# Dot products of the modulation vectors: their products into the next weight tile's low half, at a set rate per tile and stage

## The chip, the cores and the metric

The kernel runs on one core of a Trainium2 chip. The metric is the device time of one execution in microseconds. The profile shows five engines: PE (TensorE, matmuls; PEld its weight loads), DVE (VectorE), ACT (ScalarE), POOL (GpSimd) and SP (SyncE, which issues most DMAs).

## What is computed

Two transformer blocks over 256 tokens of width 1024, all in fp32. What matters here are the adaptive modulation vectors of the second block: for each of its two layers, six vectors of 1024 come from one row vector `c` and a matrix of 1024 x 6144, and for the context a shorter set from `c_ctx`.

```python
silu_c = jax.nn.silu(c)
silu_cc = jax.nn.silu(c_ctx)
for i in range(DEPTH_2):
    sh1, sc1, g1, sh2, sc2, g2 = jnp.split((silu_c @ ada_w[i] + ada_b[i])[:, None, :], 6, axis=-1)
    hx = modulate(xs, sh1, sc1)            # h * (1 + scale) + shift
    ...
    csh1, csc1, ... = jnp.split(silu_cc @ ada_w[i] + ada_b[i], 6, axis=-1)
    hc = modulate(cs, csh1, csc1)
```

The rest are matrix products with large weights: attention projections, a feed-forward pair `up` and `down`, and per layer of the second block an expert table `u`, `v` of 128 tiles each.

## The kernel before

The weights stream from HBM as tiles of 128 x 1024 fp32 (512 KB), in one fixed order, the list `items` (lines 123 to 130). The class `Stream` (line 78) does three things for a tile: `dma` issues its load on SP into one of three `raw` buffers (line 89); `split` writes a high half on ACT (line 103) and the rest, raw minus high, on DVE (line 104) into one of three `hi` and three `lo` buffers; `next` hands the pair to a matrix product, after it has issued loads up to four tiles ahead and splits up to one tile ahead. Each product is then three matmul passes: high by high, high by low, low by high.

The stages around the change, in order of time: cqkv, qk, uq, ukv, vg (4, 8, 2, 1, 8 tiles) with attention between them; five tiles of kc; wout (8) with the residual add and norm of lines 642 to 648 behind it; three more tiles of kc; up (44 tiles, `gemm_T` at line 229, each followed by `conv`, line 657, whose two DVE steps at 662 and 663 read PSUM); down (22, `gemm_N` at line 247) with the same kind of add and norm (lines 680 to 688); vc; the projections abq, abgu, abk, abgv; a second vc; then the two layers, each with u and v tiles (matmuls at line 1095 and 1158). In v, each tile also has its activation tile split into `w` (lines 1146 and 1147).

The modulation products are done on DVE, not on PE: the matrix lies transposed in HBM as tiles of 128 output columns by 1024, and one `scalar_tensor_tensor` (line 338) multiplies such a tile by the silu row and sums along the row, a dot product for each of 128 partitions. There are 16 for the context (`actx`), 48 for layer 0 (`ada0`) and 48 for layer 1 (`ada1`). The products themselves are not needed, only the sums; before, they overwrite the loaded tile. `ada_gen` (line 332) is a generator: one step issues the next load into one of three slots, the next step does the dot of the tile before. `fill(n)` (line 206) takes `n` such steps, with a fraction carried along in `debt`; the matrix products call it after each tile with `nfill` (1.3 in the first stage, 1 in wout, 0.75 in up, 1.5 in down, 1 later), so two steps make one dot. `fill_until` finishes what is left where the sums are needed.

The order in which instructions stand in each engine's queue is not the order of the program text alone. The kernel is built with `schedule_with_timeline_sim=True` (line 1333): a planner orders each queue by program order among what it reckons to be ready, and puts waits where a buffer or a value is needed. A step whose inputs are ready early can be moved ahead of program text before it. Each engine then works its queue in order.

Of the kernel before, what the change touches and what calls it, by code (L numbers as in the profile page):

```python
# [17 lines left out]
ALU = mybir.AluOpType  # L18
# [16 lines left out]
DA0, DA1 = 2, 13  # L35
NF1 = 1.3
TWO_PI = 2.0 * math.pi
# [8 lines left out]
def tile_two_blocks(ctx: ExitStack, tc: tile.TileContext, T, out):  # L46
    nc = tc.nc
# [9 lines left out]
    def nm(s):  # L57
        uid[0] += 1
        return f"{s}{uid[0]}"
# [18 lines left out]
    class Stream:  # L78
# [14 lines left out]
        def split(self, upto):  # L93
            while self.nsp < min(upto, len(self.items)):
                i = self.nsp
                w = self.items[i][1].shape[1]
                r = self.raw.pop(i)
                if i in self.own:
                    h, l = self.own.pop(i)[:2]
                else:  # L100
                    h = hi_pool.tile([128, 1024], F32R, tag="hi", name=nm("hi"))
                    l = lo_pool.tile([128, 1024], F32R, tag="lo", name=nm("lo"))
                ACT.activation(h[:, :w], r[:, :w], AF.Copy)  # L103
                DVE.tensor_sub(l[:, :w], r[:, :w], h[:, :w].bitcast(F32))  # L104
                self.hl[i] = (h, l)
                self.nsp += 1
# [95 lines left out]
    fillers = deque()  # L202

    debt = [0.0]

    def fill(n=1, tag="b"):
        debt[0] += n
        n, debt[0] = int(debt[0]), debt[0] % 1.0
        while n > 0 and fillers:
            try:  # L210
                next(fillers[0][1])
                n -= 1
            except StopIteration:
                fillers.popleft()

    def fill_until(key):
        while any(k == key for k, _ in fillers):
            try:
                next(fillers[0][1])
            except StopIteration:  # L220
                fillers.popleft()
# [6 lines left out]

    def gemm_T(name, n, xt, evac, tag="b", per=8, nfill=0, first=0):
# [17 lines left out]
    def gemm_N(name, nk, width, segs, xt, tag, per=1, nfill=0, tail=1, sqrt=False, evac=None, own=(), turn=0):  # L247

# [5 lines left out]
        for t0 in range(0, nt - tail + 1):  # L254
# [4 lines left out]
            for n in range(2):  # L259
# [71 lines left out]

    def ada_gen(layer, tiles, row, dst, slot):

        ahead = deque()

        def dot():
            c, r = ahead.popleft()
            DVE.scalar_tensor_tensor(r, r, 1.0, row(), op0=ALU.mult, op1=ALU.mult, accum_out=dst[:, c : c + 1])  # L338
            if c % 8 == 7:
                d = dst[:, c - 7 : c + 1]  # L340
                DVE.tensor_add(d, d, col(f"ada_b{layer}", c - 7, c + 1))
# [12 lines left out]

# [19 lines left out]
    with ExitStack() as b1:  # L374
# [9 lines left out]
        with ExitStack() as at:  # L384
# [42 lines left out]

            acc = gemm_N("cqkv", 8, 416, [(0, 416)], views(hT), "b", per=2, nfill=NF1)
            ssq = sm(4)
# [42 lines left out]

            acc_qk = gemm_N("qk", 8, 1024, seg2, views(hT), "a", nfill=NF1)


            def uq_evac(n, acc):
                for i in range(2):
# [4 lines left out]

            gemm_N("uq", 2, 768, [(0, 384), (384, 768)], views((cT[:, 0], cT[:, 1])), "b", tail=2, nfill=NF1,
                   evac=uq_evac)
# [7 lines left out]

            gemm_N("ukv", 1, 1024, seg2, ((lambda k: cT[:, 0, 2]), (lambda k: cT[:, 1, 2])), "b", nfill=NF1,
                   evac=ukv_evac)
# [80 lines left out]

            acc = gemm_N("vg", 8, 1024, seg2, views(hT), "a", nfill=NF1)
            vr = pa.tile([128, 1024], F32, name="vr", tag="cv").rearrange("p (n f) -> p n f", n=2)
# [58 lines left out]
        silu[0] = silu_row(p1.tile([128, D], F32, name="silu"), 0)  # L636
        fillers.append(("ada0", ada_gen(0, range(48), lambda: silu[0], adac[:, 0], slot)))
        acc = gemm_N("wout", 8, 1024, seg2, views(hT), "a", nfill=1, tail=3, sqrt=True)
        junk = p1.tile([128, D], F32, name="junk1")
# [34 lines left out]

        gemm_T("up", 44, viewsT(hT), conv, nfill=0.75)
        acc = gemm_N("down", 22, 1024, [(0, 512), (512, 1024)], views(gT), "a", nfill=1.5, tail=3, sqrt=True)
        fnw = p1.tile([128, D], F32, name="fnw")
        bcast_row(fnw, T["final_norm_w"])
        xn = p1.tile([128, 2, D], F32, name="xn2", tag="xn")
        for n in range(2):  # L680
            for i in range(2):
# [14 lines left out]
             scr=lambda: pf.tile([128, 2, 256], F32, tag="t", name=nm("t")))  # L696
        acc = gemm_N("vc", 8, 1024, [(0, 512), (512, 1024)], views(chT), "a", nfill=1)
        for n in range(2):
# [74 lines left out]
    with ExitStack() as b2:  # L773
# [53 lines left out]
        gv = pb.tile([128, 2, 512], F32, name="gv")  # L827
        acc_q = gemm_N("abq", 8, 1024, seg2, xv8, "a", nfill=1)
        acc_u = gemm_N("abgu", 8, 512, [(0, 512)], xv8, "b", per=2, nfill=1)
        qk_rope(acc_q, 0)  # L830
        acc_k = gemm_N("abk", 8, 1024, seg2, xv8, "a", nfill=1)
        for n in range(2):
            ACT.activation(gu[:, n], acc_u[n][0], AF.Gelu_apprx_tanh)
        acc_v = gemm_N("abgv", 8, 512, [(0, 512)], xv8, "b", per=2, nfill=1)
        qk_rope(acc_k, 1)
# [81 lines left out]
        for i in range(LEAD):  # L917
            scores(i)
        acc = gemm_N("vc", 8, 1024, seg2, xv8, "a", nfill=1)
        for n in range(2):  # L920
# [28 lines left out]
    def peer(layer, hT, nxt):  # L949
        with ExitStack() as pe_ctx:  # L950
# [159 lines left out]
            if layer == 0:  # L1110
# [9 lines left out]
                silu1 = silu_row(places[3], 0)  # L1120
                fillers.append(("ada1", ada_gen(1, range(48), lambda: silu1, adac[:, 1], place)))
            acc = [[bank("a") for _ in range(2)] for _ in range(2)]
            flat1 = lambda a, b: A1[:, a:b].rearrange("p j t -> p (j t)")
            for j0 in range(0, 129 - TAIL):
# [26 lines left out]
                for n in range(2):  # L1151
# [194 lines left out]
```

## Time and profile before

| | us |
|---|---|
| median of three timed runs | 2383.87 (2383.73 to 2384.34) |
| the profiled execution | 2381.28 |
| its span, first to last instruction | 2379.5 |
| PE busy in the span | 2257.6 (95%) |
| DVE busy | 1839.2 (77%) |
| ACT busy | 1323.3 (56%) |

A profile's busy time of PE comes from pipelined matmuls with modelled ends, so it is read together with the number of matmuls in a stretch. PEclk is the granted clock of TensorE as a share of its full speed. The idle time of an engine counts only where another engine waits for what it does next, so a stage is read by what ends the last wait in it.

### The profile page before, as it was taken

How to read it: one execution, taken by the hardware profiler on the slowest of the kernel's cores; microseconds unless marked ns; L12 is line 12 of the kernel's file. 1: busy time of each engine (PE TensorE's matmuls, PEld its weight loads, DVE VectorE, ACT ScalarE, POOL GpSimd, SP SyncE). 2: the span in 40 equal slices, each digit the busy share in tenths (PEclk: the TensorE clock that was granted, in tenths of full speed). 3: DMA queues.
4: the chain of work that ended last, by engine and by line, in shares of the span. 5: the costliest groups of instructions: out<-in, count | busy, mean ns of one | idle time of the engine just before them, and what ended most of it. 6: DMA issues, size and time to landing. Idle time of an engine off the chain costs nothing.

```text
span 2379.5 us, 40021 instructions
## 1 busy us (share of the span) xinstructions
PE 2257.6 (95%) x14710; PEld 2017.7 (85%) x14710; DVE 1839.2 (77%) x3679; ACT 1323.3 (56%) x2509; POOL 309.3 (13%) x359
## 2 busy tenths in 40 slices
PE   6886999999899999999999998799999999999998
PEld 6785898776699999998778887699999999888886
DVE  7879875768699957898996666789967898555565
ACT  4634554456444548876555553435547877555553
POOL 1000110211112401121000002411321112000000
PEclk9998999999899999999999999899999999999999
DMA  9559655750445554446995663444554444555663
GB/s 320 177 182 325 224 185 173 238 173 28 138 165 176 180 184 160 153 159 253 367 343 195 221 205 132 142 151 165 182 187 162 157 156 156 187 191 187 209 219 104
DMA packets 124309, 452.80 MB, mean 190 GB/s; under 512 B 13904, under 2 KB 13920, under 8 KB 123728
## 3 DMA queue, kind: packets, MB, share of 16 engines
q1 hardware_dynamic: 121104, 438.23, 53.2%
q0 software_dynamic: 3008, 12.02, 1.5%
q8 instruction: 115, 1.88, 0.3%
q14 instruction: 82, 0.67, 0.1%
HBM read 449.14 MB, written 1.05 MB: 189 GB/s over the span
## 4 chain that ended last, share of the span: by engine, by line
PE 82%; DVE 9%; DMA 3%; issue 2%; ACT 2%; POOL 1%; SPq 0%; DVEq 0%; ACTq 0%; POOLq 0%
PE pb L1158 29%; PE pb L273 10%; PE pb L1095 10%; PE pb L1096 9%; PE pb L1097 9%; PE pb L240 3%; PE pb L241 3%; PE pb L242 3%; DVE lo L104 2%; DVE araw L338 1%; PE pb L1073 1%; PE pb L1074 1%; DMA araw<-in_ada_wT 1%; POOL oh L1025 1%; ACT hi L103 1%
## 5 line engine op out<-in xcount | busy, mean ns | idle before, releaser
L104 DVE TENSOR_TENSOR lo<-raw,hi 128x1024 fp32r<-128x1024 f32 (+1 forms) x700 | 868.6, 1242 | 280.4 <-ACT hi L103 279.3
L103 ACT ACTIVATE hi<-raw 128x1024 fp32r<-128x1024 f32 (+1 forms) x700 | 739.5, 1058 | 557.4 <-PE pb L1096 245.5
L1095 PE MATMUL pb<-hTh,hi 128*128 128x256 f32 x2048 | 589.2, 288 | 1.4 <-ACT A L1099 1.4
L1097 PE MATMUL pb<-hTh,lo 128*128 128x256 f32 x2048 | 578.5, 283 | 0.6 <-DVE lo L104 0.6
L1096 PE MATMUL pb<-hTl,hi 128*128 128x256 f32 x2048 | 578.7, 283 | 0.0
L1158 PE MATMUL pb<-hi,w 128*128 128x512 f32 x1952 | 535.0, 395 | 1.1 <-ACT w L1146 1.1
L1158 PEld LDWEIGHTS pb<-hi,w 128*128 128x128 f32 x1952 | 366.4, 188 | 90.3 <-ACT w L1146 1.6
L1095 PEld LDWEIGHTS pb<-hTh,hi 128*128 128x128 f32 x2048 | 391.8, 191 | 2.2 <-ACT A L1099 2.0
L1097 PEld LDWEIGHTS pb<-hTh,lo 128*128 128x128 f32 x2048 | 391.2, 191 | 1.4 <-DVE lo L104 1.3
L1096 PEld LDWEIGHTS pb<-hTl,hi 128*128 128x128 f32 x2048 | 392.0, 191 | 0.0
L1158 PE MATMUL pb<-lo,w 128*128 128x512 f32 x976 | 307.2, 395 | 1.4 <-DVE lo L104 1.3
L1146 ACT ACTIVATE w<-A 128x256 fp32r<-128x256 f32 x252 | 104.4, 417 | 263.2 <-PE pb L1158 260.1
L1158 PEld LDWEIGHTS pb<-lo,w 128*128 128x128 f32 x976 | 182.8, 188 | 47.3 <-DVE lo L104 3.5
L240 PE MATMUL pb<-hTh,hi 128*128 128x256 f32 x672 | 192.9, 290 | 17.7 <-DVE u L663 17.7
L241 PE MATMUL pb<-hTl,hi 128*128 128x256 f32 x672 | 194.7, 291 | 1.1 <-DVE hTl L314 1.1
L242 PE MATMUL pb<-hTh,lo 128*128 128x256 f32 x672 | 192.4, 288 | 0.9 <-DVE lo L104 0.9
L1147 DVE TENSOR_TENSOR w<-A,w 128x256 fp32r<-128x256 f32 x252 | 107.2, 427 | 99.0 <-PE pb L1158 96.7
L1070 ACT ACTIVATE oh<-oj,gf 128x128 f16<-128x128 f16 x512 | 162.7, 395 | 0.0
L240 PEld LDWEIGHTS pb<-hTh,hi 128*128 128x128 f32 x672 | 131.4, 197 | 19.6 <-issue 13.6
L1109 POOL TENSOR_TENSOR A<-A,tmp 128x4 f32<-128x4 f32 (+42 forms) x128 | 83.2, 650 | 447.7 <-ACT A L1081 447.7
L241 PEld LDWEIGHTS pb<-hTl,hi 128*128 128x128 f32 x672 | 131.8, 196 | 2.2 <-DVE hTl L314 2.2
L242 PEld LDWEIGHTS pb<-hTh,lo 128*128 128x128 f32 x672 | 131.7, 196 | 1.3 <-DVE lo L104 1.3
(435 smaller groups left out, 3090.0 us busy)
## 6 DMA issues: line engine op xcount, KB each, us to landing
raw<-in_u SPq DMA_DIRECT2D x256, 512.0 KB, 3.5
raw<-in_v SPq DMA_DIRECT2D x248, 512.0 KB, 4.2
araw<-in_ada_wT SPq DMA_DIRECT2D x64, 512.0 KB, 5.1
spare<-in_ada_wT SPq DMA_DIRECT2D x48, 512.0 KB, 5.4
raw<-in_up SPq DMA_DIRECT2D x44, 512.0 KB, 3.5
raw<-in_wq SPq DMA_DIRECT2D x32, 512.0 KB, 3.6
raw<-in_down SPq DMA_DIRECT2D x22, 512.0 KB, 3.5
raw<-in_vc SPq DMA_DIRECT2D x16, 512.0 KB, 3.5
```

The source lines that it names most:

```text
L103: ACT.activation(h[:, :w], r[:, :w], AF.Copy)
L104: DVE.tensor_sub(l[:, :w], r[:, :w], h[:, :w].bitcast(F32))
L240: PE.matmul(p, h[:, kk[1]], xh(done, k), start=(k == 0), stop=False)
L241: PE.matmul(p, h[:, kk[1]], xl(done, k), start=False, stop=False)
L242: PE.matmul(p, l[:, kk[1]], xh(done, k), start=False, stop=(k == per - 1))
L273: PE.matmul(acc[n][i][:, : b - a], w, r[:, s * width + a : s * width + b], start=(k == f0 and lhs is xh and r is h), stop=(k == f1 and lhs ...
L1070: ACT.activation(row(oh, c), row(oj, c), AF.Copy, scale=gf[:, t0 + c : t0 + c + 1])
L1095: PE.matmul(p, h[:, ks], xh(0, k), start=(k == 0), stop=False)
L1096: PE.matmul(p, h[:, ks], xl(0, k), start=False, stop=False)
L1097: PE.matmul(p, l[:, ks], xh(0, k), start=False, stop=(k == 7))
L1147: DVE.tensor_sub(wl, aj, wh.bitcast(F32))
L1158: PE.matmul(acc[n][i], lhs[:, ns], r[:, i * 512 : i * 512 + 512], start=(j == 0 and lhs is wh and r is h), stop=(j == 127 and lhs is wl))
```

## The change

The generator becomes an object whose `step` issues a load and, once three tiles are on the way, does the dot of the oldest, so one step is one dot and two loads run ahead. `fill` is called from `Stream.split`, before a tile is split, with the name of the tile's weight and the lo buffer that the tile is going to use; a table `PACE` gives the dots per tile by weight. The dot writes its products into that lo buffer instead of over its own input; the subtraction of line 104 then writes the buffer as before. The calls of `fill` behind the tiles go, and with them `nfill`. Weights that are not in the table (kc, wout, the second layer's, and u, pin and so on) get no dots.

```diff
-NF1 = 1.3
+PACE = {"cqkv": 1, "qk": 1, "uq": 1, "ukv": 1, "vg": 1, "up": 0.25, "down": 1.25,
+        "vc": 0.5, "abq": 1, "abgu": 1, "abk": 1, "abgv": 1, "v0": 0.5}
...
                     l = lo_pool.tile([128, 1024], F32R, tag="lo", name=nm("lo"))
+                fill(self.items[i][0], l)
                 ACT.activation(h[:, :w], r[:, :w], AF.Copy)
                 DVE.tensor_sub(l[:, :w], r[:, :w], h[:, :w].bitcast(F32))
...
-    def fill(n=1, tag="b"):
-        debt[0] += n
-        n, debt[0] = int(debt[0]), debt[0] % 1.0
-        while n > 0 and fillers:
-            try:
-                next(fillers[0][1])
-                n -= 1
-            except StopIteration:
+    def fill(name, junk):
+
+        debt[0] += PACE.get(name, 0.0)
+        while debt[0] >= 1.0:
+            debt[0] -= 1.0
+            if fillers and not fillers[0][1].step(junk):
                 fillers.popleft()
...
-            fill(nfill)
...
-            fill(nfill * len(last), "b" if tag == "a" else "a")
...
-    def ada_gen(layer, tiles, row, dst, slot):
-
-        ahead = deque()
-
-        def dot():
-            c, r = ahead.popleft()
-            DVE.scalar_tensor_tensor(r, r, 1.0, row(), op0=ALU.mult, op1=ALU.mult, accum_out=dst[:, c : c + 1])
+    class AdaDots:
+
+
+        def __init__(self, layer, n, row, dst, slot):
+            self.layer, self.left, self.row, self.dst, self.slot = layer, deque(range(n)), row, dst, slot
+            self.ahead = deque()
+
+        def step(self, junk=None):
+
+            if self.left:
+                c, r = self.left.popleft(), self.slot()
+                nc.sync.dma_start(r, T["ada_wT"][self.layer, c])
+                self.ahead.append((c, r))
+                if self.left and len(self.ahead) < 3:
+                    return True
+            c, r = self.ahead.popleft()
+            DVE.scalar_tensor_tensor(r if junk is None else junk, r, 1.0, self.row(), op0=ALU.mult, op1=ALU.mult,
+                                     accum_out=self.dst[:, c : c + 1])
             if c % 8 == 7:
...
-        for c in tiles:
-            r = slot()
-            nc.sync.dma_start(r, T["ada_wT"][layer, c])
-            ahead.append((c, r))
-            yield
-            if len(ahead) > 1:
-                dot()
-            yield
-        dot()
+            return bool(self.left or self.ahead)
...
-        fillers.append(("actx", ada_gen(0, range(16), lambda: siluc, adacc, slot)))
+        fillers.append(("actx", AdaDots(0, 16, lambda: siluc, adacc, slot)))
...
-            acc = gemm_N("cqkv", 8, 416, [(0, 416)], views(hT), "b", per=2, nfill=NF1)
+            acc = gemm_N("cqkv", 8, 416, [(0, 416)], views(hT), "b", per=2)
...
-        gemm_T("up", 44, viewsT(hT), conv, nfill=0.75)
-        acc = gemm_N("down", 22, 1024, [(0, 512), (512, 1024)], views(gT), "a", nfill=1.5, tail=3, sqrt=True)
+        gemm_T("up", 44, viewsT(hT), conv)
+        acc = gemm_N("down", 22, 1024, [(0, 512), (512, 1024)], views(gT), "a", tail=3, sqrt=True)
...
-                fill(1)
         return hT
```

## Rows read from the trace of the kernel before

**Rows 1.** Page, busy tenths in 40 slices of the span (59.5 us each).

```profile
PE   6886999999899999999999998799999999999998
...
DVE  7879875768699957898996666789967898555565
```

**Rows 2.** Table by stretch: start:end, us, busy us (instructions), clock, DMA share, GB/s.

```profile
22.00:54.00 32.00, 31.01 (x140) 26.29 (x139) 31.22 (x85) 13.53 (x22) 1.84 (x2) 0.96 0.89 308
160.00:253.00 93.00, 61.09 (x422) 57.49 (x421) 88.90 (x158) 39.77 (x63) 7.02 (x5) 0.87 0.91 323
253.00:343.50 90.50, 90.50 (x744) 90.50 (x744) 69.22 (x111) 55.23 (x92) 11.88 (x16) 0.98 0.54 186
343.50:402.40 58.90, 58.90 (x256) 47.78 (x256) 27.66 (x26) 25.12 (x27) 0.74 (x1) 1.00 0.55 188
1125.00:1225.00 100.00, 99.90 (x427) 79.59 (x426) 94.90 (x152) 50.59 (x72) 0.00 (x0) 1.00 0.99 371
1240.00:1440.00 200.00, 200.00 (x859) 160.91 (x858) 124.03 (x152) 114.19 (x155) 1.12 (x2) 1.00 0.62 206
```

**Rows 3.** Source view of line 338, 150 to 330 us: min/median/max ns, starts.

```profile
L338 DVE SCALAR_TENSOR_TENSOR araw<-araw,silu x40: 1203/1220/1764, 159.3 to 250.6; 128x1024 f32<-128x1024 f32 x40
```

**Rows 4.** Timeline of SP's queue: start us, us, engine, line, issues, count.

```profile
182.31 19.72 SPq L347 DMA_DIRECT2D araw<-in_ada_wT  x11
...
331.60 59.44 SPq L89 DMA_DIRECT2D raw<-in_down  x22
```

**Rows 5.** Chain, 136 to 260 us: by line; first, longest, last araw wait.

```profile
by line: DMA araw<-in_ada_wT 19.6%; DVE araw L338 18.8%; PE pb L273 11.9%; DVE lo L104 9.8%; issue 8.4%; PE pb L240 6.0%; PE pb L241 5.4%; PE pb L242 5.1%; DVE u L662 2.9%; ACT hi L103 2.6%; DVE u L663 2.1%; DVE hTl L306 1.4%; PE pb L599 1.
...
160.53 3.45 DMA araw<-in_ada_wT
...
211.65 5.71 DMA araw<-in_ada_wT
...
237.67 5.10 DMA araw<-in_ada_wT
```

**Rows 6.** Waits of PE, from 0, 130, 400 us: total, times, longest.

```profile
PE pb L273 <- ACT hTh L305: 3.6, 1, 3.6
...
PE pb L240 <- DVE u L663: 17.7, 7, 4.8
...
PE pb L273 <- ACT vall L700: 5.6, 1, 5.6
```

**Rows 7.** Groups by line: shapes, count | busy us, mean ns | idle before.

```profile
L104 DVE TENSOR_TENSOR lo<-raw,hi 128x1024 fp32r<-128x1024 f32 (+1 forms) x700 | 868.6, 1242 | 280.4 <-ACT hi L103 279.3
...
L1147 DVE TENSOR_TENSOR w<-A,w 128x256 fp32r<-128x256 f32 x252 | 107.2, 427 | 99.0 <-PE pb L1158 96.7 <-ACT w L1146 2.4
...
L338 DVE SCALAR_TENSOR_TENSOR araw<-araw,silu 128x1024 f32<-128x1024 f32 x48 | 59.8, 1260 | 13.8 <-ACT silu L326 10.2 <-DMA araw<-in_ada_wT 3.4
...
L338 DVE SCALAR_TENSOR_TENSOR spare<-spare 128x1024 f32<-128x1024 f32 x16 | 19.5, 1219 | 3.2 <-ACT spare L326 3.2
```

**Rows 8.** Table by stretch for line 240 alone: columns PE and PEld.

```profile
253.00:343.50 90.50, 70.64 (x248) 48.17 (x247) 0.98 0.54 186
```

**Rows 9.** Timeline of all engines at wout's end: start us, us, engine, line.

```profile
161.57 1.22 DVE L338 SCALAR_TENSOR_TENSOR araw<-araw,silu 128x1024 f32<-128x1024 f32 x1
...
163.99 0.50 PE L273 MATMUL pb<-lo,hTh 128*128 128x512 f32 x1 [1.49 <-DVE lo L104]
...
165.72 0.39 PE L273 MATMUL pb<-hi,hTl 128*128 128x512 f32 x1
```

**Rows 10.** Timelines of DVE and POOL behind down.

```profile
404.55 2.48 DVE L683 TENSOR_TENSOR xs<-xs,pb 128x512 f32<-128x512 f32 x4
...
412.64 0.75 DVE L687 TENSOR_SCALAR xn<-xs,sm 128x1024 f32<-128x1024 f32 x1
...
425.60 0.59 POOL L178 DMA_DIRECT2D silu<-in_c_rows  x1 [8.81 <-issue]
```

**Rows 11.** Table by stretch, 184 to 188 us.

```profile
184.00:188.00 4.00, 1.54 (x6) 1.18 (x7) 3.04 (x11) 0.00 (x0) 0.00 (x0) 0.50 1.00 401
```

**Rows 12.** Timeline of DVE at the start, the third dot.

```profile
22.90 1.21 DVE L338 SCALAR_TENSOR_TENSOR araw<-araw,kT 128x1024 f32<-128x1024 f32 x1
```

More of the change, by code (lines that the diff above doesn't have):

```diff
@@ L217, in fill_until @@
         while any(k == key for k, _ in fillers):
-            try:
-                next(fillers[0][1])
-            except StopIteration:
+            if not fillers[0][1].step():
                 fillers.popleft()
@@ L227, in mm3, with gemm_T @@
         PE.matmul(p, ll, rh, start=False, stop=last)
-    def gemm_T(name, n, xt, evac, tag="b", per=8, nfill=0, first=0):
+    def gemm_T(name, n, xt, evac, tag="b", per=8, first=0):
         xh, xl = xt
@@ L244, in gemm_T, with gemm_N @@
                 done += 1
-            fill(nfill)
-    def gemm_N(name, nk, width, segs, xt, tag, per=1, nfill=0, tail=1, sqrt=False, evac=None, own=(), turn=0):
+    def gemm_N(name, nk, width, segs, xt, tag, per=1, tail=1, sqrt=False, evac=None, own=(), turn=0):
         xh, xl = xt
@@ L330, in tile_two_blocks @@
     adacc = cst.tile([128, 16], F32, name="adacc")
-    def ada_gen(layer, tiles, row, dst, slot):
-        ahead = deque()
-        def dot():
-            c, r = ahead.popleft()
-            DVE.scalar_tensor_tensor(r, r, 1.0, row(), op0=ALU.mult, op1=ALU.mult, accum_out=dst[:, c : c + 1])
+    class AdaDots:
[12 more added lines that the diff above has]
+                                     accum_out=self.dst[:, c : c + 1])
             if c % 8 == 7:
-                d = dst[:, c - 7 : c + 1]
-                DVE.tensor_add(d, d, col(f"ada_b{layer}", c - 7, c + 1))
+                d = self.dst[:, c - 7 : c + 1]
+                DVE.tensor_add(d, d, col(f"ada_b{self.layer}", c - 7, c + 1))
                 if c // 8 in (1, 4):
                     DVE.tensor_scalar(d, d, 1.0, None, ALU.add)
-        for c in tiles:
-            r = slot()
-            nc.sync.dma_start(r, T["ada_wT"][layer, c])
-            ahead.append((c, r))
-            yield
-            if len(ahead) > 1:
-                dot()
-            yield
-        dot()
+            return bool(self.left or self.ahead)
     def ada(layer, part):
@@ L471, in tile_two_blocks @@
             ROPE = DVE
-            acc_qk = gemm_N("qk", 8, 1024, seg2, views(hT), "a", nfill=NF1)
+            acc_qk = gemm_N("qk", 8, 1024, seg2, views(hT), "a")
             def uq_evac(n, acc):
@@ L481, in uq_evac @@
                          trig[:, 0, n, 32:48], trig[:, 1, n, 32:48], 4, 16)
-            gemm_N("uq", 2, 768, [(0, 384), (384, 768)], views((cT[:, 0], cT[:, 1])), "b", tail=2, nfill=NF1,
+            gemm_N("uq", 2, 768, [(0, 384), (384, 768)], views((cT[:, 0], cT[:, 1])), "b", tail=2,
                    evac=uq_evac)
@@ L491, in ukv_evac @@
                     DVE.tensor_copy(vm[:, n, i * 4 : i * 4 + 4], a3[:, :, 64:])
-            gemm_N("ukv", 1, 1024, seg2, ((lambda k: cT[:, 0, 2]), (lambda k: cT[:, 1, 2])), "b", nfill=NF1,
+            gemm_N("ukv", 1, 1024, seg2, ((lambda k: cT[:, 0, 2]), (lambda k: cT[:, 1, 2])), "b",
                    evac=ukv_evac)
@@ L573, in tile_two_blocks @@
                                rs[:, :, None].to_broadcast([128, 8, 64]))
-            acc = gemm_N("vg", 8, 1024, seg2, views(hT), "a", nfill=NF1)
+            acc = gemm_N("vg", 8, 1024, seg2, views(hT), "a")
             vr = pa.tile([128, 1024], F32, name="vr", tag="cv").rearrange("p (n f) -> p n f", n=2)
@@ L636, in tile_two_blocks @@
         silu[0] = silu_row(p1.tile([128, D], F32, name="silu"), 0)
-        fillers.append(("ada0", ada_gen(0, range(48), lambda: silu[0], adac[:, 0], slot)))
-        acc = gemm_N("wout", 8, 1024, seg2, views(hT), "a", nfill=1, tail=3, sqrt=True)
+        fillers.append(("ada0", AdaDots(0, 48, lambda: silu[0], adac[:, 0], slot)))
+        acc = gemm_N("wout", 8, 1024, seg2, views(hT), "a", tail=3, sqrt=True)
         junk = p1.tile([128, D], F32, name="junk1")
@@ L696, in tile_two_blocks @@
              scr=lambda: pf.tile([128, 2, 256], F32, tag="t", name=nm("t")))
-        acc = gemm_N("vc", 8, 1024, [(0, 512), (512, 1024)], views(chT), "a", nfill=1)
+        acc = gemm_N("vc", 8, 1024, [(0, 512), (512, 1024)], views(chT), "a")
         for n in range(2):
@@ L827, in tile_two_blocks @@
         gv = pb.tile([128, 2, 512], F32, name="gv")
-        acc_q = gemm_N("abq", 8, 1024, seg2, xv8, "a", nfill=1)
-        acc_u = gemm_N("abgu", 8, 512, [(0, 512)], xv8, "b", per=2, nfill=1)
+        acc_q = gemm_N("abq", 8, 1024, seg2, xv8, "a")
+        acc_u = gemm_N("abgu", 8, 512, [(0, 512)], xv8, "b", per=2)
         qk_rope(acc_q, 0)
-        acc_k = gemm_N("abk", 8, 1024, seg2, xv8, "a", nfill=1)
+        acc_k = gemm_N("abk", 8, 1024, seg2, xv8, "a")
         for n in range(2):
             ACT.activation(gu[:, n], acc_u[n][0], AF.Gelu_apprx_tanh)
-        acc_v = gemm_N("abgv", 8, 512, [(0, 512)], xv8, "b", per=2, nfill=1)
+        acc_v = gemm_N("abgv", 8, 512, [(0, 512)], xv8, "b", per=2)
         qk_rope(acc_k, 1)
@@ L918, in tile_two_blocks @@
             scores(i)
-        acc = gemm_N("vc", 8, 1024, seg2, xv8, "a", nfill=1)
+        acc = gemm_N("vc", 8, 1024, seg2, xv8, "a")
         for n in range(2):
@@ L1120, in peer @@
                 silu1 = silu_row(places[3], 0)
-                fillers.append(("ada1", ada_gen(1, range(48), lambda: silu1, adac[:, 1], place)))
+                fillers.append(("ada1", AdaDots(1, 48, lambda: silu1, adac[:, 1], place)))
             acc = [[bank("a") for _ in range(2)] for _ in range(2)]
```

## The prediction

> **What bounds the kernel now.** I read the slices of the page first: TensorE is busy nearly everywhere, and the deepest dip behind the start is the fourth slice, 178 to 238 us, six tenths, where VectorE is at nine instead [rows 1]. Then the table by stage: from 253 us on, TensorE is busy without a gap; from 160 to 253 us it does 422 matmuls in 93 us, at a mean granted clock of 0.87, while VectorE is busy 88.90 of 93 us and the DMA 0.91 of the time [rows 2]. What fills VectorE there are the dot products: the source view of their line shows 40 of them between 159.3 and 250.6 us [rows 3]. In the code they are spread over wout, up and down at half a dot or less per tile; on the chip they run together, because nothing holds a dot except its own load and the queue order is made by a planner when the kernel is built. SP's queue shows the same: eleven modulation loads in one run at 182.3 us, no weight load between [rows 4]. In the chain of waits this stretch is a sequence of "three dots, then a wait for the next load": five such waits for araw, from 3.45 to 5.71 us, 24.3 us together (19.6% of the 124 us shown), with dots, subtractions and conv steps in line between them [rows 5]. So the stretch is bound by a VectorE queue that stands still for loads of 512 KB, with conv's reads of PSUM queued behind: TensorE waited 17.7 us for them [rows 6].
>
> Elsewhere dots cost little. In the v0 stage 48 dots run at about one per tile, the DMA is busy 0.99 of the time at 371 GB/s, and still TensorE does 427 matmuls in 100 us, against 859 in 200 us where no dot is left [rows 2].
>
> **The change, part by part.**
>
> *The output moves into the low half of the tile about to be split.* The arithmetic is the same instruction over 1024 elements, so its price stays: 1.22 us [rows 3]. What is new is a wait: a dot is now the first writer of that lo buffer, so it cannot start before TensorE has finished with the tile three places earlier. The planner can no longer pull it ahead; dots run at the set rate. Queued behind the waiting dot is the subtraction of that tile, which had to wait for the same buffer already; it now ends one dot later. With three lo buffers TensorE has two whole tiles in hand: 2 x 2.68 us in down (58.90 us for 22 tiles), of which dot and subtraction take 1.22 + 1.24 = 2.46 us [rows 2, 3, 7]. I cost the wait itself at nothing; if that cover were gone, each dot would add up to its own 1.22 us.
>
> *wout loses its dots, up gets 0.25 per tile.* This is the main term. up needs 44 tiles. From 253 to 343.5 us, without dots, 248 matmuls of line 240 are 31 tiles: 2.92 us each [rows 8]. VectorE there is busy 69.22 of 90.5 us, 2.23 per tile; a quarter of a dot makes 2.54, below 2.92 [rows 2]. So up should run at TensorE's pace: 44 x 2.92 = 128.5 us. Its start: wout's last matmul begins at 165.72 us, after 1.49 us in which TensorE waited for a subtraction that stood behind three dots, the last of them at 161.57 [rows 9]; without them it ends about 164.5. The norm that follows can be read from the same code after down: first residual add 404.55, xn 412.64, which is 8 us [rows 10]; the transposes and their evacuations I put at 4 us more, eight pieces of about half a microsecond. wout's first adds can begin some 3 us before its end, so up's first input stands at about 174 to 175 us. The three kc tiles (3 x 2.92 = 8.8 us) fill TensorE meanwhile. That gives up's end at 175 + 128.5 = 303.5 us instead of 343.5: 40 us. I take off 1 us for a clock drop in a shorter gap than now (from 184 to 188 us, with 6 matmuls in 4 us, the granted clock is 0.50, the lower level of 1.2 GHz [rows 11]): **-39 us**. Bounds: at most -42, where TensorE goes from wout to kc to up without a gap; at least -24.3, the five load waits alone.
>
> *down gets 1.25 per tile.* 27 dots land here, where none ran before. VectorE: 1.24 + 1.25 x 1.22 = 2.77 by means, but v0 shows how tightly these pack: there 1.24 + 0.43 + 1.22 = 2.89 by means were done in 94.9/35.6 = 2.67 per tile; scaled so, down needs 2.56 of 2.68 [rows 2, 7]. The DMA: 2.25 loads of 0.524 MB per tile at 371 GB/s are 3.18 us, more than 2.68: a deficit of 0.50 x 22 = 11 us if nothing were loaded ahead. But the weight loads run about four tiles ahead (down's first issue is at 331.60, its first matmul at 343.5 [rows 2, 4]) and three modulation tiles wait in their slots, so what must land during the stage for its last tile is some 17 weight and 21 modulation tiles: 38 x 1.41 = 53.7 us, plus about 5 us from the last landing to the last matmul. That is 58.7, just the present 58.9. I take **+2 us** for gaps in the queue, bounds 0 and +11. Here a page of the Trainium skill speaks against the change: "DMA: Bandwidth & Descriptors", Specifications, gives about 358 GB/s as the limit of one core's share of HBM. By it the 38 loads would take 55.7 us, an estimate from that figure, and the term would be +4. The trace holds 371 GB/s over 100 us and 401 over 4 us [rows 2, 11], so I keep the measured rate.
>
> *vc and the projections behind it.* vc gets 4 dots, abq finishes with about 8. In before TensorE stands 5.6 us behind vc, because ScalarE's queue holds the evacuation of vall behind the second silu row, whose load starts at 425.60, when the pools of the first block are given back [rows 6, 10]. The last dots in vc's loop now read the first silu row later (before, all of that row's readers were done by 251 us), which could push that load by 3 to 4 us; or the planner, seeing it later, puts the evacuation first and the 5.6 us vanish. I take **0**, bounds -5.6 and +4.
>
> *First stage, 0 to 160 us.* One dot per tile instead of about two thirds, the same 16 dots. VectorE is nearly full in its first half in any case (from 22 to 54 us it is busy 31.22 of 32 [rows 2]), so moving a dot inside it gives little. Three dots now stand among the first hTl pieces, the last at 22.90, while TensorE waits 3.6 us for the first hT [rows 6, 12]; there will be one at most. **-1 us**, bounds -5 and +5.
>
> *v0.* Half a dot per tile: 48 dots over about 100 tiles instead of the first 48. TensorE lost 0.6% there over 130 us, 0.8 us, and VectorE stood 3.2 us for the silu row at the start [rows 2, 7]. **-1 us**, bounds 0 and -3.
>
> Two loads ahead instead of one, and one step per dot: no instruction more, the loads (112) and dots (112) are the same.
>
> **Sum.** -39 + 2 + 0 - 1 - 1 = -39 us. The profiled execution took 2381.28 us with a span of 2379.5; it becomes 2342.3. The median of the three timed runs is 2383.87, 2.6 us more, so the forecast is **2345 us**.
>
> **Rivals.**
> 1. *The waits move along.* If the dots of the paced stages wait for loads as often as now (24.3 us over 40 dots, 0.6 each [rows 3, 5]), the 51 dots of the first stage, down and abq give back 31 us: -8, so 2376. For it: a slot's load is issued only three steps of 2.14 us ahead in down, and the waits in the chain run up to five or six. Against: v0 ran at the same DMA saturation without loss.
> 2. *Slower.* The dot stands in front of the subtraction that feeds TensorE, in one queue. Its place is down and the early stage with their busy DMA: six loads in flight are 8.5 us by 1.41 each, 3.2 later than the 5.3 us a load has. If every dot came 3.2 us late, two tiles in hand (2.9 us left after dot and subtraction) hide part where one dot falls on a tile, and only 1.7 us where two do. The loss is 0.3 to 1.5 us per dot; it decides from 0.8 us on each of 51 dots, which is the 39 to 41 us gained. At 1.5 it costs 77 us: about 2422.
> 3. *It does not do what it says.* The planner still bunches dots in up, since the loads on SP are not paced: no change, 2384. Against: the buffer is a hard dependency.
>
> **How the numbers follow.** The forecast case gets 0.86, rival 1 0.08, rival 2 0.04, rival 3 0.02. The bounds of the terms together give 2329 to 2382; their ends don't fall together, so I take **2331 to 2362**, the first with most of the gains in vc and the first stage, the second with up at -30 and down at +7; it leaves out rivals 1 to 3 and some of the forecast's own edge. About 0.2% is what a measurement of this kernel can tell from no change. Faster 0.94 (forecast and rival 1), same 0.02, slower 0.04.
>
> **What would show it.** Right: no dot between wout's end and up's third tile group; dots one by one in front of a subtraction, some 9 in up and 27 in down; no five-microsecond pieces of araw loads in the chain; up at 2.9 us per tile from its start; DMA near 0.99 in down. Wrong on down: TensorE idle there behind subtractions, tiles above 2.9 us. Wrong on the main term: up's start still near 190 us, or up's tiles above 3 us.

## The result and the profile after

The changed kernel takes 2357.58 us (median of four timed runs, 2354.97 to 2358.79), the ratio to the kernel before is 0.9893 with an interval from 0.9881 to 0.9904. That is 26 us less where 39 were forecast, inside the range of 2331 to 2362 and 13 us above the forecast. The profiled execution took 2357.86 us with a span of 2356.1, so in the frame of the profiles the gain is 23.4 us. In the changed kernel the dot stands in line 345, its load in line 340, the weight loads in line 91, the splits in lines 106 and 107, `gemm_T`'s matmuls in 239 to 241, `gemm_N`'s in 271.

The page's slices of the changed kernel, in 40 parts of the span, answer to [rows 1]. The fourth slice has risen from six to nine tenths; the eighth, 412 to 471 us, has come down from nine to eight:

```profile
PE   7899999899799999999999998799999999999998
...
DVE  7867899678799957897877867889957898555565
```

The same kind of table by stretch as [rows 2] (start:end, length, busy us and instructions of PE, PEld, DVE, ACT and POOL, granted clock, DMA share, GB/s). The stretches follow the changed kernel's stages: up from 184 us, down, vc with abq, and the first of the two in v0 that stand in [rows 2]:

```profile
184.00:313.00 129.00, 129.00 (x1059) 128.65 (x1059) 106.64 (x174) 79.56 (x131) 28.85 (x20) 0.99 0.64 208
310.00:380.00 70.00, 66.28 (x289) 51.73 (x288) 63.78 (x93) 27.34 (x31) 1.47 (x2) 1.00 0.96 364
380.00:442.00 62.00, 51.63 (x211) 40.73 (x210) 50.67 (x81) 27.79 (x34) 12.37 (x9) 0.92 0.74 257
1125.00:1225.00 100.00, 100.00 (x432) 81.17 (x431) 80.34 (x115) 52.91 (x73) 0.00 (x0) 1.00 0.85 284
```

In up TensorE is busy for the whole 129 us. In down it is not (66.28 of 70), and the DMA is at 0.96. In vc with abq 10 of 62 us are lost, and that with the DMA at 0.74 only.

The source view of the dot's line from 150 to 330 us answers to [rows 3], and SP's timeline to [rows 4]: 18 dots begin there instead of 40, the first at 211.9 (8 before 300 us; from 305 to 384 us there are 30), and one load of a modulation tile follows four weight loads, where eleven went in one run:

```profile
L345 DVE SCALAR_TENSOR_TENSOR lo<-araw,silu x18: 1207/1215/1486, 211.9 to 329.4; 128x1024 fp32r<-128x1024 f32 x18
...
224.80 0.33 SPq L340 DMA_DIRECT2D araw<-in_ada_wT  x1
226.32 8.87 SPq L91 DMA_DIRECT2D raw<-in_up  x4
236.41 0.33 SPq L340 DMA_DIRECT2D araw<-in_ada_wT  x1
```

What TensorE waited for, with total, times and longest, first from 130 to 254 us and then from 380 to 442 us, answers to [rows 6]. The 17.7 us for `u` are gone and no dot has a part in what is left before up; the 5.6 us for `vall` have become 0.2, and in their place stand 8.8 us for subtractions:

```profile
PE pb L295 <- DVE xn L647: 2.8, 1, 2.8
PE pb L295 <- DVE mixed L611: 1.4, 1, 1.4
PE pb L295 <- DVE hTl L303: 0.9, 1, 0.9
...
PE pb L271 <- DVE lo L107: 8.8, 3, 6.9
...
PE pb L271 <- ACT vall L699: 0.2, 1, 0.2
```

For the account by stage I took from both traces the start of the first and of the last matmul of each stage (a stage is known by its matmuls' line and their number). "Shift" is the change of the last one, so the steps between shifts are what each stage gives or takes:

| stage | before, us | after, us | shift of its end | step | forecast of the step |
|---|---|---|---|---|---|
| vg | 69.5 to 99.4 | 69.9 to 104.1 | +4.7 | +4.7 | -1 (whole first stage) |
| wout | 136.9 to 165.7 | 142.3 to 168.7 | +2.9 | -1.8 | about -1 |
| up | 192.8 to 343.2 | 184.6 to 313.3 | -29.9 | -32.8 | about -38 |
| down | 343.6 to 404.7 | 309.8 to 379.6 | -25.0 | +4.9 | +2 |
| vc | 405.4 to 429.3 | 379.9 to 409.4 | -19.9 | +5.1 | 0, with abq |
| abq | 435.3 to 459.7 | 409.6 to 441.4 | -18.3 | +1.6 | |
| v0 | 1100.0 to 1460.2 | 1081.8 to 1438.8 | -21.4 | -3.1 | -1 |
| the end | | | -23.4 | -2.0 | 0 |

The steps of the first three rows are forecast together at -40; they came to -29.9.

### The profile page after: what moved, and what is told of

Its sections match the earlier page's. It is cut to its first block, busy times and chain, and to the rows that moved or that the text cites. A ratio compares the mean times of both kernels' runs of the same rounds, so it can differ in the third digit from the quotient of the medians.

```text
span 2356.1 us, 40089 instructions
## 1 busy us (share of the span) xinstructions
PE 2254.9 (96%) x14710; PEld 2016.6 (86%) x14710; DVE 1839.4 (78%) x3679; ACT 1320.2 (56%) x2509; POOL 318.1 (14%) x359
## 4 chain that ended last, share of the span: by engine, by line
PE 72%; DVE 6%; POOL 1%; issue 1%; ACT 1%; DMA 1%; DVEq 0%; POOLq 0%; ACTq 0%
PE pb L1157 30%; PE pb L1094 9%; PE pb L1095 9%; PE pb L1096 9%; PE pb L271 6%; PE pb L240 1%; PE pb L1072 1%; PE pb L239 1%; PE pb L241 1%; PE pb L1073 1%; DVE lo L107 1%; POOL oh L1024 1%; PE pb L972 1%; PE pb L875 0%; DVE sm L876 0%
## 5 line engine op out<-in xcount | busy, mean ns | idle before, releaser
L1145 ACT ACTIVATE w<-A 128x256 fp32r<-128x256 f32 x252 | 104.1, 416 | 253.5 <-PE pb L1157 250.8
L240 PE MATMUL pb<-hTl,hi 128*128 128x256 f32 x672 | 192.8, 288 | 1.7 <-DVE hTl L311 1.6
```

## Experiments

Each was timed beside the kernel before, which was timed anew in every set of runs: its median was 2383.8 us beside the changed kernel, 2380.5 beside the first four experiments, 2381.4 beside the next four and 2381.2 beside the last. So a difference of two medians from different sets can be off by some 3 us, and the ratio to the kernel before is given with each. "In place" means that a dot's products go over its own load, as in the kernel before. The stage times in this section are read like the table above.

**Is it the buffer, or the new rates and the second load ahead?** One word of the change is undone:

```diff
-            if fillers and not fillers[0][1].step(junk):
+            if fillers and not fillers[0][1].step():
```

> The changed kernel with its rates, its place in program order and its two loads ahead, but each dot writes its products over its own input again, so that no lo buffer holds it. Theory A (the lo buffer is what holds the dots back): the planner bunches them as before, 34 behind up's first splits, and the time goes back to 2375 to 2386 us, up's end to about 340 us with waits for araw of about five microseconds in the chain. Rival B (the rates, and two loads ahead instead of one, do it): the time stays at 2355 to 2362, without such waits.

Measured: 2381.97 us, ratio 1.0006 [0.9997, 1.0016]. The source view of the dot's line (150 to 340 us), the first line of the chain of waits (136 to 260 us) and TensorE's longest wait there (130 to 330 us) are those of the kernel before [rows 3, 5, 6], almost to the digit:

```profile
L345 DVE SCALAR_TENSOR_TENSOR araw<-araw,silu x41: 1208/1220/1761, 159.9 to 253.4; 128x1024 f32<-128x1024 f32 x41
...
by line: DMA araw<-in_ada_wT 18.5%; DVE araw L345 16.6%; PE pb L271 12.0%; DVE lo L107 9.2%; issue 7.9%; PE pb L239 7.4%; PE pb L240 6.2%; PE pb L241 6.0%; ACT hi L106 3.4%; DVE u L661 2.7%; DVE u L662 2.3%; PE pb L598 1.7%; DVE hTl L303 1.
...
PE pb L239 <- DVE u L662: 17.7, 6, 6.0
```

The program text asks for a quarter of a dot per tile in up, and the planner still puts 41 dots between 159.9 and 253.4 us. So rates and lookahead do nothing by themselves; the gain needs the output buffer, which ties a dot to its tile. What the buffer would give with the old rates was not run.

**The first stage.** Only its 16 context dots go in place:

```diff
-            if fillers and not fillers[0][1].step(junk):
+            if fillers and not fillers[0][1].step(None if fillers[0][0] == "actx" else junk):
```

> The changed kernel, only the 16 dots for the context write over their own input again; all others as changed. Theory A (the first stage lost about 5 us because its dots now stand in front of subtractions and come later): wout starts again at about 137 us instead of 142.3, total 2351 to 2354. Rival B (the first stage's loss has nothing to do with the buffer): wout's start and the total stay, 2357 to 2359.

Measured: 2358.21 us, 0.9909 [0.9886, 0.9932]. The time is that of the rival. wout starts 3.0 us earlier, at 139.3, up 1.3 us earlier, at 183.3 (by the experiment with v0's dots below, that is within the spread of single executions), and up ends at 313.1 as in the changed kernel (313.3). So at least 3.0 of the 5.4 us by which wout came later are the dots' (vg takes 30.4 us instead of 34.2, and 29.9 before), but they are taken up before up ends. The table by stretch from wout's last matmul to up's first, first of the changed kernel, then of this one, shows where: the gap is 1.1 us longer and the granted clock in it is lower, 0.85 instead of 0.87. In both the clock drops to 0.5, the 1.2 GHz level, from the gap on into up's first matmuls, for 6.8 us in the one and 10.2 in the other:

```profile
168.70:184.60 15.90, 12.16 (x90) 11.42 (x89) 12.57 (x25) 11.42 (x20) 0.00 (x0) 0.87 0.60 199
```

```profile
166.30:183.30 17.00, 12.18 (x90) 11.42 (x90) 13.10 (x27) 11.18 (x20) 0.00 (x0) 0.85 0.63 193
```

**down's rate.** Six dots are moved from down to up:

```diff
-PACE = {..., "up": 0.25, "down": 1.25,
+PACE = {..., "up": 0.375, "down": 1,
```

> The changed kernel with 0.375 dots per tile in up and 1 in down instead of 0.25 and 1.25; the sum over both stages is the same. Theory A (down's 2.25 loads per tile are more than the DMA brings, which cost 5 us): down falls from 69.9 to 62 to 65 us from first to last matmul, up stays within 1 us of 128.7, total 2352 to 2355. Rival B (VectorE in up cannot take half a dot more every four tiles): up grows by 3 us or more and the total stays or rises, 2357 to 2362. Rival C (down is slow for another reason): nothing moves.

Measured: 2354.11 us, 0.9889 [0.9872, 0.9905]. By the medians that is 3.5 us below the changed kernel, by the ratios 1.0, and the intervals lie over each other: a gain in the whole is not shown. The stages show one. down takes 64.8 us instead of 69.9, as the first theory had it, and up 131.4 instead of 128.7, more than it allowed; at vc's end 9.7 us are gained. At abq's end 3.6 are left: TensorE's longest wait for a subtraction (in this view of 300 to 445 us) lies there and has grown from 6.9 to 11.2 us:

```profile
PE pb L271 <- DVE lo L107: 12.0, 3, 11.2
PE pb L271 <- ACT vall L699: 1.5, 1, 1.5
```

**No dots in vc and abq.** The eleven dots there go to the stages behind them:

```diff
-        "vc": 0.5, "abq": 1, "abgu": 1, "abk": 1, "abgv": 1, "v0": 0.5}
+        "vc": 0, "abq": 0, "abgu": 1, "abk": 1, "abgv": 1, "v0": 0.5}
```

> The changed kernel with no dots in vc and abq; what is left of the 48 goes into abgu and abk at one per tile. Theory A (the dots in vc fill VectorE while the norm runs, and those in abq stand in the queue waiting for the second silu row with subtractions behind them, which cost 5 and 7 us): vc falls from 29.6 to about 24 us, abq from 31.7 to about 24.5, and the gap of 5.6 us before abq stays away or comes back: total 2345 to 2353. Rival B (silu's row itself blocks, whatever the dots do): abq stays near 30, total 2355 to 2359.

Measured: 2349.28 us, 0.9872 [0.9855, 0.9888], below the changed kernel by 8.3 us of the medians and by 5.0 of the ratios, inside the range of the first theory; vc takes 25.9 us and abq 27.1, against 29.6 and 31.7 (23.9 and 24.4 in the kernel before). TensorE's waits from 370 to 436 us:

```profile
PE pb L271 <- ACT vall L699: 3.6, 1, 3.6
PE pb L271 <- DVE lo L107: 1.9, 3, 0.8
```

The long wait for a subtraction is gone and the wait for `vall` is back in part. abq ends 9.0 us earlier; the dots, now in abgu and abk, cost 1.6 there (11.6 and 24.1 us, 11.1 and 23.0 without dots).

**One load ahead instead of two.**

```diff
-                if self.left and len(self.ahead) < 3:
+                if self.left and len(self.ahead) < 2:
```

> One dot stands loaded ahead instead of two, everything else as in the changed kernel (2357.6 us). Theory A (the buffer that a dot writes is what the change is worth; a loaded tile lies ready long before its dot): 2355 to 2360, up 128 to 130 us long. Theory B (the second tile ahead hides the load of 1.4 to 6 us): the dots of the first stage and of down wait for their loads, and the time is 2363 to 2372.

Measured: 2361.35 us, 0.9913 [0.9896, 0.9929], between the two expectations; its interval overlaps that of the changed kernel. up takes 129.9 us. In the first stage uq takes 8.2 us instead of 5.0, but wout ends as early as in the changed kernel (168.1 against 168.7). In down dots waited 3.7 us for loads (2.6 in the changed kernel). The second load ahead may be worth 4 to 5 us (3.8 by the medians, 4.8 by the ratios) and may be worth nothing; that stays open.

**Both better rates together.**

```diff
-PACE = {..., "up": 0.25, "down": 1.25, "vc": 0.5, "abq": 1, ...
+PACE = {..., "up": 0.375, "down": 1, "vc": 0, "abq": 0, ...
```

> Rates: up 0.375 instead of 0.25, down 1 instead of 1.25, and none in vc and abq. Theory A (the losses in down and in vc with abq are separate, each by its own queue): both gains add, down 64 to 66 us long, vc 26, abq 27, the time 2357.6 - 5 - 8 = 2344 to 2347. Theory B (dots moved into up cost there what down gives back, with TensorE's clock or VectorE as the bound): about the time without dots in vc and abq alone, 2348 to 2351.

Measured: 2346.22 us, 0.9853 [0.9837, 0.9870], the lowest median of all. It is 11.4 us below the changed kernel by the medians, where the two edits apart gave 3.5 and 8.3, and 9.5 by the ratios (apart 1.0 and 5.0). Here the intervals of the two kernels lie apart; with intervals of about 4 us to each side the two gains add as far as can be told. down 65.1, vc 25.1, abq 24.7. The table by stretch of this run, up, down and vc:

```profile
184.00:313.00 129.00, 128.62 (x1047) 127.16 (x1047) 110.46 (x180) 78.92 (x129) 26.45 (x21) 0.99 0.71 227
312.00:376.00 64.00, 63.65 (x284) 51.10 (x282) 54.86 (x79) 27.72 (x30) 3.12 (x2) 1.00 0.97 358
376.00:402.00 26.00, 25.04 (x114) 19.70 (x113) 23.27 (x38) 14.17 (x20) 6.51 (x4) 1.00 0.57 183
```

up loses 12 matmuls in 129 us by the higher rate, 1047 against 1059 (1.1%, about 1.5 us); VectorE's busy time has gone from 106.64 to 110.46.

**Still fewer in down.** The same with down at 0.8, so four dots more fall behind abq:

```diff
-PACE = {..., "down": 1,
+PACE = {..., "down": 0.8,
```

> As the run with up 0.375, down 1 and none in vc and abq, but down at 0.8: four loads of 0.5 MB fewer in down, four dots more in the stages behind abq. Theory A (down is bound by DMA, 1.4 us for each load): down 4 x 1.4 = 5.6 us shorter than with rate 1, 59 to 60 us, and the time 2339 to 2343 unless the stages behind abq give it back. Theory B (at rate 1 down is no longer bound by DMA alone): down within 2 us of that run, time 2344 to 2348.

Measured: 2352.27 us, 0.9881 [0.9864, 0.9897], 6 us slower than the run before it and outside both ranges. down takes 64.0 instead of 65.1 us, so four loads less are worth 1.1 us, not 5.6: of down the second theory holds, at rate 1 it is no longer bound by the DMA alone. Two things were lost. abgv takes 15.9 us instead of 11.1. And ScalarE's queue behind vc has again the order of the kernel before: its timeline (start, us, engine, line; in brackets what it waited for) shows the evacuation of `vall` behind the silu row, which cost TensorE 4.8 us, while the second timeline, of the faster run, has the evacuation first:

```profile
402.05 1.28 ACT L323 ACT_TABLE_LOAD   x1 [4.07 <-DMA silu<-in_c_rows]
403.34 1.06 ACT L323 ACTIVATE silu<-silu 128x1024 f32<-128x1024 f32 x1
...
405.25 1.06 ACT L699 ACTIVATE vall<-pb 128x512 f32<-128x512 f32 x2
```

```profile
401.09 1.07 ACT L699 ACTIVATE vall<-pb 128x512 f32<-128x512 f32 x2
...
407.70 1.28 ACT L323 ACT_TABLE_LOAD   x1 [4.59 <-DMA silu<-in_c_rows]
```

**v0's dots.** Only they go in place:

```diff
-            if fillers and not fillers[0][1].step(junk):
+            if fillers and not fillers[0][1].step(None if name == "v0" else junk):
```

> The 48 dots of v0 alone write over their own load again, all others as in the changed kernel. Theory A (what v0 gained, 3.1 us, comes from where its dots write): v0 359 to 361 us long and the time 2359.5 to 2362. Theory B (it comes from the state in which v0 starts, or from where its loads are issued): v0 356 to 358 and the time 2356 to 2359.

Measured: 2356.92 us, 0.9896 [0.9879, 0.9912], and in its profiled execution, the slowest of the four at 2360.51, v0 takes 358.4 us (357.0 in the changed kernel, 360.2 before). The time is that of the second theory: v0's gain doesn't need the buffer. By the stage's length, which lies between the two theories, 1.4 of the 3.1 us could be the buffer's, but v0 in the runs with the buffer there varies from 356.4 to 358.5, so that can't be told. The dots bunch here as in the kernel before, with the DMA at 0.96 and VectorE at 94.89 us [rows 2]:

```profile
1125.00:1225.00 100.00, 99.92 (x428) 79.89 (x427) 94.89 (x151) 51.58 (x72) 0.00 (x0) 1.00 0.96 360
```

This run also shows how far two executions differ. Up to v0 every engine's queue holds the same instructions in the same order as in the changed kernel, and still wout ends 1.6 us earlier (167.1), up starts 1.1 us earlier (183.5) and vc takes 27.9 us instead of 29.6. A difference of less than 2 us between the stages of two traces therefore says nothing by itself.

**Best rates and context dots in place.** The edit of the second experiment on top of the fastest kernel:

> The rates of the run with up 0.375, down 1 and none in vc and abq (2346.2 us), and the 16 dots of the first stage write over their own load again. Theory A (the delay of the first stage is real and reaches the end): wout starts 3 us earlier, at 139, and the time is 2342 to 2344. Theory B (it is taken up between wout and the end of up, as in the changed kernel): wout starts 3 us earlier, up ends at 313 to 315 all the same, and the time is 2345 to 2348.

Measured: 2347.72 us, 0.9862 [0.9845, 0.9878], the same as without it. wout starts 4.6 us earlier (137.3), ends 2.4 earlier, up starts 1.5 and ends 1.6 earlier, abq ends 0.8 earlier, and at the end nothing is left. The first stage's delay is real and costs next to nothing, as in the second experiment.

## Why the forecast was right in its main mechanism and 13 us off in size

**The cause of the dip.** Right in what the output buffer does: without it the dots bunch and the dip is back, as the run with the dots in place shows, and with it the waits for `u` vanish. Wrong in one reading: VectorE did not stand still for loads. It was busy for 88.90 of the 93 us [rows 2], and of its own waits from 130 to 254 us in the kernel before only 3.4 us, in eight pieces, were for the loads of dots:

```profile
DVE araw L338 <- DMA araw<-in_ada_wT: 3.4, 8, 0.7
```

So the five pieces of the chain, 24.3 us together, are for the most part loads in flight while VectorE worked on other things. More than half of its 93 us were the dots themselves, 40 x 1.22 = 48.8 us, in the same queue as conv's steps. The sum of the forecast doesn't use this reading; its lower bound for up (-24.3) and the price of rival 1 (0.6 us per dot) do. The bounds of the terms also add up to 2328 and 2380, not to 2329 and 2382.

**up's pace.** Right: 44 x 2.92 = 128.5 us were forecast, 128.7 measured, with VectorE busy 106.64 / 44 = 2.42 us per tile (forecast 2.54). The limit of that cover shows too: at 0.375 dots per tile it is 2.51, and up takes 130.7 to 131.8 us in four runs, against 128.7 to 129.9 in five at 0.25.

**up's start.** This is the term that was mis-sized: 184.6 us instead of 175. One to two of these 9.6 us are the spread of single executions: in five other runs whose queues have the same order up to 200 us, up starts between 182.0 and 183.5. The rest has two parts. The first stage came 5.4 us later to wout (forecast -1, bound +5). A dot that cannot be pulled ahead sits where the text puts it. The last context dot ended at 71.2 us, 3.9 later than before (67.4), with vg's subtractions behind it. The forecast held that moving them inside a full VectorE queue gives little, and did not ask what they displace. That alone explains little of the miss, though: in two experiments it was taken back in part or whole and up's end moved 0.2 and 1.6 us, no more than the spread. The rest is the stretch from wout's last matmul to up's first. 15.9 us were measured, and 10.5 (164.5 to 175) allowed: the forecast took 8 us for the adds and the norm and 4 for transposes and evacuations, and let the first adds begin 3 us before wout's end. VectorE's timeline of the changed kernel shows the chain take 12.0 us from the first add to the start of xn of the second half, the piece that the forecast had at 8. Five subtractions of other tiles stand in the queue between its links, the first two of them here, where behind down in the kernel before there was one. TensorE's transposes and the evacuations follow:

```profile
167.97 0.68 DVE L643 TENSOR_TENSOR xs<-xs,pb 128x512 f32<-128x512 f32 x1
168.57 1.22 DVE L107 TENSOR_TENSOR lo<-raw,hi 128x1024 fp32r<-128x1024 f32 x1
169.70 1.88 DVE L643 TENSOR_TENSOR xs<-xs,pb 128x512 f32<-128x512 f32 x3
171.49 1.22 DVE L107 TENSOR_TENSOR lo<-raw,hi 128x1024 fp32r<-128x1024 f32 x1
...
179.92 0.75 DVE L647 TENSOR_SCALAR xn<-xs,sm 128x1024 f32<-128x1024 f32 x1
```

And the first add came 0.7 us before wout's last matmul started, not 3. What bounds this gap when wout comes earlier is not settled: it grows by 1.1 and 0.9 us in the two experiments, with a longer spell at the low clock in both (10.2 us, against 6.8).

**down.** Right in kind, +4.9 instead of +2, inside the bounds. By its share the DMA is the limit from 325 us on. The table by stretch inside down:

```profile
315.00:325.00 10.00, 8.01 (x33) 5.88 (x33) 9.50 (x16) 3.41 (x6) 0.73 (x1) 1.00 0.86 303
325.00:335.00 10.00, 10.00 (x44) 8.11 (x43) 8.46 (x16) 3.44 (x4) 0.00 (x0) 1.00 0.97 351
345.00:355.00 10.00, 10.00 (x45) 8.03 (x44) 9.08 (x13) 4.25 (x4) 0.00 (x0) 1.00 1.00 396
365.00:380.00 15.00, 14.53 (x62) 10.94 (x60) 14.15 (x21) 6.89 (x7) 0.00 (x0) 1.00 1.00 381
```

Who waited for whom from 310 to 376 us: ScalarE's split waited 21.4 us for weight tiles to land, and now and then TensorE for the subtraction behind it:

```profile
ACT hi L106 <- DMA raw<-in_down: 21.4, 11, 3.6
...
PE pb L271 <- DVE lo L107: 3.7, 5, 1.6
```

The rate was hardly the error: over the 70 us of the stage it is 364 GB/s, against the 371 that the forecast used, and in the later rows here 381 to 396. The limit of the Trainium skill ("DMA: Bandwidth & Descriptors", Specifications, about 358 GB/s) does not hold here: the whole stage runs above it, at 364. That its +4 is nearer to the +4.9 is a coincidence. The "HBM Reference" of the Trainium skill, Specifications (TRN2), says that a core that streams alone gets well above that share. With that the trace agrees, at 396 GB/s over 10 us.

The error was in what was loaded ahead. The forecast had 38 loads to land between down's start and its last tile, 17 of weights and 21 of modulation tiles. In the trace 42 land between up's last matmul (313.3 us) and the landing of the last weight tile (373.8), 19 and 23, because three weight tiles and not five were there when up ended. They took 60.5 us, and 5.8 us later the last matmul began: 66.3 us in all, against the 58.7 that the forecast worked out (in the kernel before it is 61.5 by the same measure). Four loads by 1.41 are 5.6 us of the difference. In the kernel before the first weight load went out 12 us ahead of the matmuls; now it is 8.4 (301.42 to 309.8), and from then on weight and modulation loads take turns on SP. The experiment that takes 5.5 dots out of down won 5.1 us there, about 1 us for each, and brought the time from up's last matmul to down's to 61.4 us: the term was gone, and four dots fewer gave nothing clear of the spread. A dot less is a load less and 1.22 us of VectorE less, so this experiment alone does not tell the two apart.

**vc and abq.** The step that failed. Forecast 0 with +4 as the bound, measured +6.7. Both things that the forecast named came, and they do not exclude each other: the evacuation of `vall` goes first and the gap behind vc closes, and the load of the second silu row waits for the last dot that reads the first. POOL's and VectorE's timelines show the rest of the way:

```profile
407.12 0.59 POOL L181 DMA_DIRECT2D silu<-in_c_rows  x1 [13.44 <-DVE lo L345]
...
415.95 1.23 DVE L345 SCALAR_TENSOR_TENSOR lo<-araw,silu 128x1024 fp32r<-128x1024 f32 x1 [5.42 <-ACT silu L323]
...
419.60 3.49 DVE L107 TENSOR_TENSOR lo<-raw,hi 128x1024 fp32r<-128x1024 f32 x3
```

The load goes out only at 407.12, behind the dot at 405.35, and the row is ready at 415.9. By then abq has begun, and its dots, at one per tile, read that row. VectorE stands 5.42 us before the first of them; two more dots (417.10 and 418.25) and three subtractions are queued behind it, and TensorE waits 6.9 us for a subtraction that had no need of the row. The kernel before had the same order, three dots that wait for the row with the subtraction of abq's second tile behind them:

```profile
433.81 1.23 DVE L338 SCALAR_TENSOR_TENSOR araw<-araw,silu 128x1024 f32<-128x1024 f32 x1 [5.31 <-ACT silu L326]
...
437.46 1.22 DVE L104 TENSOR_TENSOR lo<-raw,hi 128x1024 fp32r<-128x1024 f32 x1
```

There it cost nothing of its own, since TensorE stood for `vall` in the same microseconds and began abq only at 435.3. The gap of 5.6 us behind vc hid the wait for the row; with the gap closed, abq begins 6.3 us before the row is ready and the wait shows. The forecast asked what the wait does to the silu row, but not who is queued behind the dot that reads it. Behind the stand TensorE works at a lower clock, too, 0.88 from 421 to 442 us, the second row here:

```profile
394.00:409.60 15.60, 12.98 (x51) 10.04 (x50) 15.59 (x27) 7.03 (x9) 2.48 (x4) 0.89 0.66 232
...
421.00:442.00 21.00, 21.00 (x82) 17.14 (x83) 15.37 (x24) 6.79 (x8) 0.00 (x0) 0.88 0.74 263
```

The other part, vc's own 5.6 us, goes with a full VectorE: from 394 to 409.6 us, the first row, it is busy for 15.59 of 15.60 us, and four dots stand in vc among the steps of the norm and its evacuation. In the run without these dots vc loses 3.7 of its 5.6 us and abq 4.7 of its 7.3, and abq ends 9.0 us earlier, more than the 6.7 of the miss; how much of it is the late row and how much the full VectorE, that run does not separate.

**v0 and the rest.** Forecast -1, measured -3.1, just past the bound of -3, and 2.0 more behind it. The rate shows in the DMA's share, 0.85 in the stretch from 1125 to 1225 us against 0.99 [rows 2], and TensorE does 432 matmuls instead of 427 there. In the run with v0's dots in place they bunch again (0.96, 428 matmuls) and the kernel's time is the same, so neither the buffer nor the wider spread of the loads is shown to matter here; where v0's gain and the 2 us behind it come from stays open. These 4.1 us beyond the forecast hide a part of the misses above, which come to 19.7 us (10.1 up to up's end, 2.9 in down, 6.7 in vc and abq): that the total is off by no more than this is in part luck.

**The rivals.** Rival 1 (the waits move along) is true of one place, abq, and for another reason, a common input instead of the loads: dots waited for loads for 2.6 us in down, in six pieces. That is 0.1 us per dot, as in the kernel before (3.4 us over 40 dots), and not 0.6. Rival 2 (the dot in front of the subtraction) is seen in down, where TensorE waits 3.7 us for subtractions, and only above one dot per tile: at one it waits 0.3. Rival 3 is the run with the dots in place: without the buffer as their output the planner bunches them, at 2382 us.

## What to carry to other kernels

Where a planner orders the queues, a rate in the program text is a wish; to make it hold, side work needs a dependency on the work that it should pace with, and a shared output buffer is one that costs no instruction. But what stands behind work so tied waits with it: before tying it, list for each stage what stands behind it in its in-order queue and every input it waits for, and leave the stages out in which VectorE is already full or an input comes late, since here 11 dots of 112 in two such stages cost 5 to 8 us beside a gain of 26. A wait that vanishes may only have hidden another one: look at what else ended in it. And a chain of waits that names a load does not say that the engine stood; its busy time does. Count the loads ahead in the new order of the queue rather than the old: a lead of 12 us before the change was 8 after it.

## What the runs showed of the hardware

Two VectorE instructions took about three and four times as long beside a large GpSimd instruction. In VectorE's and GpSimd's timelines of the changed kernel xn takes 0.75 us at 386.45 and 2.79 at 387.50, and a dot 3.42 us at 391.35 instead of 1.22; GpSimd's two multiplications of 128 x 1024 lie exactly there:

```profile
386.45 0.75 DVE L686 TENSOR_SCALAR xn<-xs,sm 128x1024 f32<-128x1024 f32 x1
387.50 2.79 DVE L686 TENSOR_SCALAR xn<-xs,sm 128x1024 f32<-128x1024 f32 x1
391.35 3.42 DVE L345 SCALAR_TENSOR_TENSOR lo<-araw,silu 128x1024 fp32r<-128x1024 f32 x1
...
387.33 2.41 POOL L687 TENSOR_TENSOR xs<-xn,fnw 128x1024 f32<-128x1024 f32 x1 [65.17 <-DVE sm L199]
390.42 3.26 POOL L687 TENSOR_TENSOR xs<-xn,fnw 128x1024 f32<-128x1024 f32 x1 [0.68 <-issue]
```

The first ends at 390.29, 0.55 us after GpSimd's first (389.74), and the second at 394.77, 1.1 us after GpSimd's second (393.68). "SBUF — State Buffer", Terms, of the Trainium skill speaks of a port pair that VectorE and GpSimd share and that one of them holds for a whole instruction while the other waits; the two rows fit that. So a dot in vc took 2.2 us more than its 1.22, once. The price is not the dot's own: in the run with both better rates, which has no dot there, a subtraction beside GpSimd's first multiplication (382.20 to 384.60) takes 3.21 us instead of 1.23:

```profile
382.46 3.21 DVE L107 TENSOR_TENSOR lo<-raw,hi 128x1024 fp32r<-128x1024 f32 x1 [0.40 <-ACT hi L106]
```
